# Output products in token layout, a norm as two numbers a partition, and h updated by fp32 products with a diagonal

## The chip, the cores and the metric

The kernel runs on one core of one Trainium2 chip. The metric is the device time of one execution in microseconds (us); lower is better. All inputs lie in the chip's memory (HBM) when it starts. The engines that the text speaks of are TensorE (PE; its weight loads are PEld), VectorE (DVE), ScalarE (ACT), GpSimd (POOL) and SyncE (SP, which issues the weight transfers).

## The reference, cut to what matters

Two residual blocks over 256 tokens of width 2048, all in fp32. `h` is the residual stream; every sublayer has the same frame, of which the change touches the norm ahead of it, its last product, and the update of `h`:

```
rms_norm(x, g) = x * rsqrt(mean(x*x, axis=-1) + 1e-6) * g
h = x
# block 1
z = rms_norm(h, g) @ w_in                     # then a recurrent mixer and sparse attention
h = h + rms_norm(concat(rms_norm(y_lru), rms_norm(y_nsa)) @ w_out, g)
h = h + rms_norm(square(relu(rms_norm(h, g) @ mlp_w1)) @ mlp_w2, g)
h = h + sigmoid(h @ ple_gate) * (p @ ple_proj)
# block 2: layer 0 has the mixer "sb_gla", layer 1 the mixer "s5"
for layer in 0, 1:
    y = mixer(rms_norm(h, g0))                # s5 ends in val * sigmoid(gate), (val, gate) = y @ w_glu
    h = h + rms_norm(y, g1)
    gate, up = split(rms_norm(h, g2) @ w_ffn_in)
    h = h + rms_norm((silu(gate) * up) @ w_ffn_out, g3)
```

So there are six updates of the form `h = h + rms_norm(...)` and six norms of `h` ahead of a product.

## The kernel before, in words

**Layout.** Activations lie transposed: a tile of 128 channels (partitions) by 256 tokens, 16 such tiles k = 0..15 for the width 2048. `h` is `[128, 16, 256]`. An operand of a product is split in two fp32r parts, high and low (`split`, L245 and L246, or with a gain L248 and L249), and a product is the sum of high*high, low*high and high*low.

**Products.** `wload` fetches a piece of the weights (512 KB: two k-tiles of 512 columns), ACT rounds it to `wh` (L261), DVE forms the rest `wl` (L262); there are four buffers of each. `group` makes 512 output columns of a product: for each k, weight tiles of 128x128 are the loaded operand, and the activations stream. In the wide form (used where `self.alt` is set) high and low stream together, 512 columns for `wh` and 256 for `wl`, and each output tile takes a PSUM bank of its own; in the narrow form (around the two mixers, and at the end of an output product) three products of 256 columns each. `evac` empties the banks. `outs` runs `group` four times for an output product (2048 columns); in the last call the last 512 columns are cut in two halves (`narrow`). `agroup` with `amode` is an existing third form, used for a few products in the mixers (L751 to L753): there the activations of 128 tokens are the loaded operand and 512 columns of weights stream, so that the output has tokens on its partitions.

**Banks.** PSUM has eight banks of 512 columns: four called `ps`, two `px`, two `pm`. `group` takes four of `ps` and `px` in a rotation of three patterns (`self.gpar`).

**The boundary between two sublayers.** The output product is evacuated in fp32 into `Y`; ACT squares each tile, DVE adds the squares (`stat`), `rnorm` sums them over partitions by fp32 products with a matrix of ones (L442), and makes the reciprocal root on a 128x256 tile with Ln and Exp on ACT and four DVE operations (L447 to L454). Twenty products without use (`fill`, L430) lie behind the L442. Then `upd(k)`: `t = Y[k] * r` (L533, on DVE, every second one on POOL) and `h[k] += t` (L534, DVE). `make_x` hands out `pre(k)`, which calls `upd(k)` and splits h[k] with the gain; the first `group` of the next sublayer calls `pre(k)` for each k, so its products wait for the tiles one after the other. The norm of the new `h` is taken behind this first group: `h_stat` squares on ACT (L381) and adds on POOL (L382), then `rnorm`, and where a number per token on partitions is wanted, `rnorm_tok` (L461, two products of one column). The result scales the evacuated products, since the norm is one factor per token.

**What sets the order.** Each engine runs its instructions in order. The order is set when the kernel is built, by priorities that follow the program; the work of `s5_gen`, which prepares tables for the s5 mixer mostly on POOL, is given a lower priority and lies between other work.

Of the kernel before, what the change touches and what calls it, by code (L numbers as in the profile page):

```python
# [18 lines left out]
P = 128  # L19
T = 256  # L20
# [115 lines left out]
class K:  # L136
# [195 lines left out]
    def outs(self, Xk, ks, W, r0, last, step=None, tags=("ps",) * 4, **kw):  # L332

        for gi in range(4):
            if step:
                step(gi)
            if not (last and gi == 3):
                yield gi * 4, self.group(Xk, ks, lambda k0: self.wload(  # L340
                    [((slice(None),), self.wsrc(W, r0 + k0 - ks[0], gi * 512))]), tag=tags[gi], **kw)
                continue
            for k in (12, 14):
                yield k, self.group(Xk, ks, lambda k0: self.wload(
                    [((slice(None),), self.wsrc(W, r0 + k0 - ks[0], k * P, 4, T))], (P, 4, T)),
                    ntile=2, kc=4, tag=tags[gi], **{**kw, "narrow": True})
# [36 lines left out]

    def stat(self, acc, y, k):

        if k < 12:
            if k == 0:
                acc.append(self.acct())
            self.sq_add(acc[0], y, k == 0)
        else:  # L390
            acc.append(self.l())
            self.last_act = self.nc.scalar.activation(acc[-1], y, AF.Square)
# [63 lines left out]
    def rnorm_tok(self, acc, n):  # L456

        nc = self.nc
        ps = self.ps()
        for c in range(2):  # L460
            nc.tensor.matmul(ps[:, c:c + 1], acc[:, c * P:(c + 1) * P], self.ones[:, 0:1], start=True, stop=True)  # L461
        v = self.s([P, 16], tag="nv")[:, :2]
        nc.vector.tensor_scalar(v, ps[:, 0:2], 1.0 / n, EPS, op0=ALU.mult, op1=ALU.add)
        r = self.rsqrt_small(v, 2)
        rt = self.s([P, 2], tag="rt")
        nc.vector.tensor_copy(rt, r)
        return rt
# [50 lines left out]
    def h_stat(self):  # L518
        acc = self.acct()
        for k in range(NK):  # L520
            self.sq_add(acc, self.h[:, k], k == 0, self.nc.gpsimd)
        return acc

    def post_norm(self, Y, acc, fill=20):

        nc = self.nc
        r = self.rtile("c")
        self.rnorm(acc, D, r, fill)

        def upd(k, engs=None):  # L530
            t = self.e()
            m, a = engs or (nc.gpsimd if k > 1 and k % 2 else nc.vector, nc.vector)
            m.tensor_tensor(t, Y[:, k], r, op=ALU.mult)  # L533
            a.tensor_tensor(self.h[:, k], self.h[:, k], t, op=ALU.add)  # L534

        return upd

    def newY(self):
        return self.xs([P, NK, T], F32)

    def put_ys(self, Y, acc, k0, ys, gain):

        for i, y in enumerate(ys):
            self.stat(acc, y, k0 + i)
        for i, y in enumerate(ys):
            self.nc.scalar.activation(Y[:, k0 + i], y, AF.Copy, scale=self.vec(gain[0], gain[1] + k0 + i))
# [90 lines left out]
    def block1_in(self):  # L637
# [10 lines left out]
        for gi in range(2):  # L648
            ps = self.group(Xk, ks, std(C_U + gi * 512), pre=pre)
            if pre:  # L650
                pre = None
                acc = self.h_stat()
                self.rnorm(acc, D, rb)
                rt = self.rnorm_tok(acc, D)
# [261 lines left out]
    def nsa_gen(self, q, ksw, vv, kcmp, VB, gt, wk):  # L916
# [141 lines left out]
        self.r_nsa = self.rtile("c")  # L1058
        self.rnorm(acc, 1024, self.r_nsa)
# [6 lines left out]
    def block1(self):  # L1066
# [10 lines left out]
        for k, ps in self.outs(lambda k: XL[:, k], list(range(8)), W, 0, False):  # L1077
            for j, p in enumerate(ps):
                self.evac(p, out=Y[:, k + j])
        acc = []  # L1080
        for k, ps in self.outs(lambda k: self.XN[:, k - 8], list(range(8, 16)), W, 8, True, tags=("ps", "ps", "px", "ps"),
                               pre=self.mix_until(self.made)):
            self.mix_end()
            ys = [self.evac(p, mul=self.r_nsa) for p in ps]
            for j, y in enumerate(ys):
                (nc.gpsimd if k < 12 else nc.vector).tensor_tensor(y, y, Y[:, k + j], op=ALU.add)
            self.put_ys(Y, acc, k, ys, ("mix_post", 0))
# [4 lines left out]
        self.upd = self.post_norm(Y, acc)  # L1092
# [4 lines left out]
    def mlp(self):  # L1097
# [3 lines left out]
        rb = self.rtile("a")  # L1101
        r2 = self.rtile("b")
        W1, W2 = I["mlp_w1"], I["mlp_w2"]
        Y = self.newY()
        accy = []
        ks = list(range(16))
        for ch in range(4):
            H = self.newX()
            self.bg_drain = ch == 3
            for gi in range(4):  # L1110
# [5 lines left out]
                if pre:  # L1116
                    pre = None
                    self.dump("h1", self.h)
                    self.rnorm(self.h_stat(), D, rb)
                    V.tensor_tensor(r2, rb, rb, op=ALU.mult)  # L1120
# [14 lines left out]
            for k, ps in self.outs(lambda k: self.xk(H, k), ks, W2, ch * 16, ch == 3, step):  # L1135
                if ch < 3:
                    for j, p in enumerate(ps):
                        self.evac(p, out=Y[:, k + j], add=Y[:, k + j] if ch else None)
                else:
                    ys = [self.evac(p, add=Y[:, k + j], mul=r2) for j, p in enumerate(ps)]  # L1140
                    self.put_ys(Y, accy, k, ys, ("mlp_post", 0))
        self.ple_proj(0, behind)
        self.upd = self.post_norm(Y, accy, 0)
        self.ple_proj(1)

# [35 lines left out]
    def finish(self):  # L1181
        nc = self.nc
        ov = self.out.rearrange("(k p) t -> p k t", p=P)
        for k in range(NK):
            self.upd(k, ((nc.vector, nc.gpsimd)[k % 3 == 2],) * 2)
# [4 lines left out]
    def mixer0(self):  # L1190
# [12 lines left out]
        for dst, c0, mul in ((gk, 3584, rb), (gq, 3072, r8)):  # L1203
            ps = self.group(Xk, ks, std(c0), pre=pre)
            if pre:
                pre = None
                hd = self.save_h()
                acc = self.h_stat()
# [816 lines left out]
```

## Time and profile before

| | |
|---|---|
| median of 3 runs | 3584.61 us (3579.72 to 3590.34) |
| the profiled execution: time | 3582.63 us |
| its span | 3580.8 us |
| its mean granted clock of TensorE | 0.986 |
| PE busy | 3460.7 us, 97% of the span, 22198 instructions |
| DVE, ACT, POOL busy | 2332.0, 1831.7, 1030.5 us |
| chain that ended last | PE 87%, DVE 6%, ACT 2% |

Read it so: PE is busy nearly all the time, and most of the chain that sets the end is PE's own stream of L304 products. The idle time that PE has lies in a few places, and its boundaries are among them.

### The profile page before, as it was taken

How to read it: one execution, taken by the hardware profiler on the slowest of the kernel's cores; microseconds unless marked ns; L12 is line 12 of the kernel's file. 1: busy time of each engine (PE TensorE's matmuls, PEld its weight loads, DVE VectorE, ACT ScalarE, POOL GpSimd, SP SyncE). 2: the span in 40 equal slices, each digit the busy share in tenths (PEclk: the TensorE clock that was granted, in tenths of full speed). 3: DMA queues.
4: the chain of work that ended last, by engine and by line, in shares of the span. 5: the costliest groups of instructions: out<-in, count | busy, mean ns of one | idle time of the engine just before them, and what ended most of it. 6: DMA issues, size and time to landing. Idle time of an engine off the chain costs nothing.

```text
span 3580.8 us, 59154 instructions
## 1 busy us (share of the span) xinstructions
PE 3460.7 (97%) x22198; PEld 3039.8 (85%) x22198; DVE 2332.0 (65%) x3610; ACT 1831.7 (51%) x2879; POOL 1030.5 (29%) x1510
## 2 busy tenths in 40 slices
PE   9999999999999999999899999999689899999998
PEld 9888888888888898999788888888578888888887
DVE  7686785567656867546766566667755765565557
ACT  5656654644445644346544444445555544444444
POOL 2231242299620113103445565556300200000000
PEclk9999999999999999999999999999899999999999
DMA  8744456667766564566577777778876466666664
GB/s 237 213 121 152 127 176 190 184 216 216 245 206 197 179 195 140 144 196 186 153 217 233 225 238 224 232 223 277 265 223 187 144 190 190 190 189 188 189 189 130
DMA packets 506167, 699.55 MB, mean 195 GB/s; under 512 B 43318, under 2 KB 317143, under 8 KB 505880
## 3 DMA queue, kind: packets, MB, share of 16 engines
q1 hardware_dynamic: 473712, 628.99, 57.2%
q0 software_dynamic: 27456, 63.65, 5.8%
q8 instruction: 174, 2.85, 0.3%
q10 hardware_dynamic: 4712, 3.13, 0.3%
q14 instruction: 113, 0.93, 0.1%
HBM read 654.17 MB, written 37.22 MB: 193 GB/s over the span
## 4 chain that ended last, share of the span: by engine, by line
PE 87%; DVE 6%; ACT 2%; DMA 2%; issue 2%; POOL 2%; SPq 0%; DVEq 0%; ACTq 0%; POOLq 0%
PE ps L304 58%; PE px L304 21%; DVE x L534 1%; DVE wl L262 1%; PE ps L751 1%; PE ps L752 1%; PE ps L753 1%; PE pm L1734 1%; ACT wh L261 1%; DVE e L533 1%; DVE x L249 1%; DMA m<-in_s5bT_dram 0%; DMA m<-in_wg_dram 0%; PE px L973 0%; PE px L1363 0%
## 5 line engine op out<-in xcount | busy, mean ns | idle before, releaser
L262 DVE TENSOR_TENSOR wl<-wr,wh 128x1024 fp32r<-128x1024 f32 x1126 | 1452.4, 1293 | 1070.1 <-ACT wh L261 1062.8
L304 PE MATMUL ps<-x,wh 128*128 128x512 f32 (+1 forms) x8000 | 2080.6, 350 | 33.0 <-DVE x L249 14.1
L261 ACT ACTIVATE wh<-wr 128x1024 fp32r<-128x1024 f32 x1126 | 1188.5, 1058 | 1291.8 <-PE ps L304 775.5
L304 PE MATMUL ps<-x,wl 128*128 128x256 f32 x6272 | 1390.2, 281 | 0.8 <-DVE wl L262 0.7
L304 PEld LDWEIGHTS ps<-x,wl 128*128 128x128 f32 x6272 | 1187.3, 190 | 205.0 <-issue 3.4
L304 PEld LDWEIGHTS ps<-x,wh 128*128 128x128 f32 x8000 | 1241.5, 191 | 52.2 <-DVE x L249 15.2
L304 PE MATMUL px<-x,wh 128*128 128x512 f32 (+1 forms) x2336 | 733.3, 395 | 16.2 <-DVE x L249 14.3
L304 PEld LDWEIGHTS px<-x,wl 128*128 128x128 f32 x2304 | 433.6, 188 | 102.6 <-issue 2.4
L304 PE MATMUL px<-x,wl 128*128 128x256 f32 x2304 | 459.1, 279 | 0.0
L304 PEld LDWEIGHTS px<-x,wh 128*128 128x128 f32 x2336 | 358.6, 189 | 28.0 <-DVE x L249 17.0
L533 POOL TENSOR_TENSOR e<-x,r_c 128x256 f32<-128x256 f32 x40 | 39.7, 997 | 1052.9 <-DVE r_c L454 1044.9
L382 POOL TENSOR_TENSOR acc<-acc,sq 128x256 f32<-128x256 f32 x89 | 78.0, 877 | 246.8 <-ACT sq L381 244.1
L1776 POOL TENSOR_TENSOR m<-m,m 128x128 f32<-128x128 f32 x128 | 69.6, 567 | 242.0 <-PE pm L1734 242.0
L365 ACT ACTIVATE e<-ps 128x256 f32<-128x256 f32 x288 | 106.1, 371 | 51.1 <-PE ps L304 47.9
L245 ACT ACTIVATE x<-e 128x256 fp32r<-128x256 f32 x168 | 67.8, 410 | 78.9 <-DVE e L1513 42.1
L367 DVE TENSOR_TENSOR e<-ps,e 128x256 f32<-128x256 f32 x256 | 105.0, 415 | 4.3 <-ACT e L365 4.3
L1793 POOL TENSOR_TENSOR m<-m,m 128x256 f32<-128x256 f32 x64 | 65.9, 1029 | 73.2 <-DMA m<-in_s5bT_dram 73.1
L246 DVE TENSOR_TENSOR x<-e,x 128x256 fp32r<-128x256 f32 x168 | 78.5, 476 | 12.5 <-ACT x L245 8.8
L1775 POOL TENSOR_TENSOR m<-m,m 128x128 f32<-128x128 f32 x128 | 76.1, 619 | 0.7
L1795 POOL TENSOR_TENSOR m<-m,m 128x256 f32<-128x256 f32 x64 | 72.6, 1134 | 0.7
L365 ACT ACTIVATE e<-px 128x256 f32<-128x256 f32 x144 | 53.4, 370 | 24.5 <-PE px L304 23.0
L751 PE MATMUL ps<-wh,x 128*128 128x512 f32 x160 | 64.4, 403 | 0.3 <-ACT wh L261 0.3
(486 smaller groups left out, 2870.0 us busy)
## 6 DMA issues: line engine op xcount, KB each, us to landing
wr<-in_w_ffn_in_dram SPq DMA_DIRECT2D x704, 256.0 KB, 3.2
wr<-in_mlp_w_dram SPq DMA_DIRECT2D x256, 512.0 KB, 4.2
wr<-in_w_ffn_out_dram SPq DMA_DIRECT2D x176, 512.0 KB, 4.5
wr<-in_w_in_dram SPq DMA_DIRECT2D x152, 512.0 KB, 3.8
wr<-in_w_out_dram SPq DMA_DIRECT2D x64, 512.0 KB, 3.8
wr<-in_w_glu_dram SPq DMA_DIRECT2D x128, 256.0 KB, 3.1
wr<-in_ple_gate_dram SPq DMA_DIRECT2D x32, 512.0 KB, 4.1
wr<-in_w_in_dram SPq DMA_DIRECT2D x32, 256.0 KB, 5.1
```

The source lines that it names most:

```text
L246: b = (eng or nc.vector).tensor_tensor(dst[:, 1], src, dst[:, 0].bitcast(F32), op=ALU.subtract)
L261: nc.scalar.activation(wh, wr, AF.Copy)
L262: nc.vector.tensor_tensor(wl, wr, wh.bitcast(F32), op=ALU.subtract)
L304: mm = lambda o, w, x, a, z: nc.tensor.matmul(o, w, x, start=a, stop=z, skip_group_check=True)
L365: a = S.activation(t, ps[:, T:2 * T], AF.Copy)
L367: self.hold = a, V.tensor_tensor(z, ps[:, 0:T], t, op=ALU.add)
L382: (eng or nc.vector).tensor_tensor(acc, acc, q, op=ALU.add)
L533: m.tensor_tensor(t, Y[:, k], r, op=ALU.mult)
L751: nc.tensor.matmul(ps, xh, wh, start=first, stop=False, skip_group_check=True)
L1775: G_.tensor_tensor(cx[:, q], u_(0), l_(0), op=ALU.mult)
L1776: G_.tensor_tensor(t1[:, q], u_(1), l_(1), op=ALU.mult)
L1795: G_.tensor_tensor(ob[:, :, ri], ob[:, :, ri], t1, op=(ALU.subtract, ALU.add)[ri])
```

## The change

`outs` no longer calls `group`, but a new function `atok`: activations of 128 tokens loaded, weights streaming, as `agroup` does (which now calls it). `Y` becomes `[128 tokens, 2 halves, 2048 channels]`. Two `ps` banks hold a group's output, emptied by one operation each (`add_up`). The squares of a token then lie along a row, and ACT's Square sums them itself (`accum_out`, `sq_sum`): the norm is two numbers on each partition. `rsqrt_tok` makes the reciprocal root on a 128x2 tile (13 DVE operations of two elements; 15 where the factor `by` comes in). `post_norm` writes it on the diagonal of two 128x128 matrices `dg`, and `upd(k)` is two fp32 products, Y's 128x128 block (loaded) with `dg` (streaming), which transpose and scale in one, into a `px` bank, and one DVE operation `h[k] += gain * pt`. The fills are gone, and POOL has no part in an update.

The norm of the new `h` (`h_norm`, at five places: both mixers' entries with `rb` and `rt`, the mlp, and both ffn) is changed too: ACT squares h[k], and two fp32 products of one column sum each square over partitions, 32 products in all. `bcast` spreads the result along a row where it is wanted (`rb`).

The diff, cut to its core:

```diff
+    def atok(self, Xk, ks, load, w, kc=2, pre=None, tag="ps"):
+        pv = [self.ps(tag)[:, 0:w] for _ in range(2)]
+        n = len(ks)
+        for a in range(0, n, kc):
...
+            wh, wl = load(ks[a])
+            for kk in range(kc):
+                for c in range(2):
+                    self.amode(pv[c], Xk(ks[a + kk]), c, wh[:, kk], wl[:, kk], a + kk == 0, a + kk == n - 1)
+            self.mix_step()
+        return pv
...
-                yield gi * 4, self.group(Xk, ks, lambda k0: self.wload(
+                yield slice(gi * 512, gi * 512 + 512), self.atok(Xk, ks, lambda k0: self.wload(
...
+    def rsqrt_tok(self, ss, n, tag="rt", by=None):
+        V = self.nc.vector
         v = self.s([P, 16], tag="nv")[:, :2]
+        if by is not None:
+            V.tensor_tensor(v, ss, by, op=ALU.mult)
+            V.tensor_tensor(v, v, by, op=ALU.mult)
+            ss = v
+        V.tensor_scalar(v, ss, 1.0 / n, EPS, op0=ALU.mult, op1=ALU.add)
         r = self.rsqrt_small(v, 2)
...
-    def h_stat(self):
-        acc = self.acct()
+    def h_norm(self, dst=None, tag="rt"):
+        nc = self.nc
+        ps = self.ps()
         for k in range(NK):
-            self.sq_add(acc, self.h[:, k], k == 0, self.nc.gpsimd)
-        return acc
+            q = self.e("sq", bufs=2)
+            self.last_act = nc.scalar.activation(q, self.h[:, k], AF.Square)
+            for c in range(2):
+                nc.tensor.matmul(ps[:, c:c + 1], q[:, c * P:(c + 1) * P], self.ones[:, 0:1], start=(k == 0 and c == 0),
+                                 stop=(k == NK - 1), skip_group_check=True)
+        rt = self.rsqrt_tok(ps[:, 0:2], D, tag)
+        if dst is not None:
+            self.bcast(rt, dst)
+        return rt
...
-    def post_norm(self, Y, acc, fill=20):
+    def post_norm(self, Y, ss, gain, by=None):
...
-        r = self.rtile("c")
-        self.rnorm(acc, D, r, fill)
-
-        def upd(k, engs=None):
-            t = self.e()
-            m, a = engs or (nc.gpsimd if k > 1 and k % 2 else nc.vector, nc.vector)
-            m.tensor_tensor(t, Y[:, k], r, op=ALU.mult)
-            a.tensor_tensor(self.h[:, k], self.h[:, k], t, op=ALU.add)
+        V.tensor_reduce(s2, ss[:, :, 0:self.ssn], axis=AX.X, op=ALU.add)
+        r = self.rsqrt_tok(s2, D, "rp", by)
+        dg = [self.s([P, P], tag="dg", bufs=2) for _ in range(2)]
+        for c in range(2):
+            V.tensor_scalar(dg[c], self.ident, r[:, c:c + 1], None, op0=ALU.mult)
+        banks = {}
+        self.gpar = 2
+
+        def upd(k, eng=None):
+            if k % 2 == 0:
+                banks[0] = self.ps("px")
+            pt = banks[0][:, (k % 2) * T:(k % 2 + 1) * T]
+            for c in range(2):
+                nc.tensor.matmul(pt[:, c * P:(c + 1) * P], Y[:, c, k * P:(k + 1) * P], dg[c], start=True, stop=True)
+            V.scalar_tensor_tensor(self.h[:, k], pt, self.vec(gain[0], gain[1] + k), self.h[:, k], op0=ALU.mult, op1=ALU.add)
...
-                    self.rnorm(self.h_stat(), D, rb)
+                    rt = self.h_norm(rb, "rf")
...
-            with self.low(-self.bg_low):
+            with self.low(-3 * self.bg_low):
```

The order of PE's instructions moves at two places. The first is the boundary from the s5 mixer's last product to the ffn of layer 1. Before (`pm` sums, `l` squares, `cst` the ones, `px` and `ps` the ffn's output, `x` the activations):

```order
L442 MATMUL pm_29733<-l_29596,cst 128x256
L442 MATMUL pm_29733<-l_29729,cst 128x256
L430 MATMUL pm_29739<-cst 128x128 x20
L304 MATMUL px_29776<-x_29770,wh_29793 128x512
L304 MATMUL px_29777<-x_29770,wh_29793 128x512
L304 MATMUL px_29776<-x_29770,wl_29794 128x256
```

Now (L788 is the third product of `amode`, L577 the update's products, whose loaded operand `x_25870` is Y):

```order
L787 MATMUL ps_27189<-wl_27287,x_25869 128x256
L788 MATMUL ps_27189<-wh_27286,x_25869 128x256
L577 MATMUL px_27363<-dg_27348,x_25870 128x128
L577 MATMUL px_27363<-dg_27349,x_25870 128x128
L577 MATMUL px_27397<-dg_27348,x_25870 128x128
L577 MATMUL px_27397<-dg_27349,x_25870 128x128
L577 MATMUL px_27363<-dg_27348,x_25870 128x128
L577 MATMUL px_27363<-dg_27349,x_25870 128x128
L577 MATMUL px_27397<-dg_27348,x_25870 128x128
L304 MATMUL ps_27359<-x_27352,wh_27377 128x512
```

The sums by ones and the fills are gone; three and a half pairs of update products stand ahead of the ffn's first product, the other twelve and a half stand among its first group.

The second place is behind this first group, where the norm of the new `h` is taken. Before, one L442 stands there, and the second group follows without a break:

```order
L304 MATMUL ps_29779<-x_29771,wl_30025 128x256 x2
L442 MATMUL pm_30091<-acc_30044,cst 128x256
L304 MATMUL ps_30131<-x_29770,wh_30138 128x512 x2
L304 MATMUL ps_30131<-x_29770,wl_30139 128x256 x2
L304 MATMUL ps_30132<-x_29770,wh_30138 128x512 x2
```

Now PE has the one-column products L542 of 15 squares there, one pair at a time between products of the second group (whose banks are `px_27758`, `px_27759`, `ps_27760` and `ps_27761`); the last four pairs:

```order
L542 MATMUL pm_27635<-cst,sq_27684 128x1 x2
L304 MATMUL ps_27760<-x_27352,wl_27789 128x256
L542 MATMUL pm_27635<-cst,sq_27688 128x1 x2
L304 MATMUL ps_27760<-x_27352,wl_27789 128x256
L304 MATMUL px_27758<-x_27352,wh_27811 128x512 x2
L542 MATMUL pm_27635<-cst,sq_27692 128x1 x2
L304 MATMUL px_27758<-x_27352,wl_27812 128x256
L542 MATMUL pm_27635<-cst,sq_27696 128x1 x2
```

and eight rows later the products that spread the norm along a row (L421), and the first product into the last of the second group's banks:

```order
L304 MATMUL px_27759<-x_27352,wh_27834 128x512 x2
L421 MATMUL pm_27722<-dg_27723,cst 128x128
L421 MATMUL pm_27722<-dg_27726,cst 128x128
L304 MATMUL px_27759<-x_27352,wl_27835 128x256 x2
L304 MATMUL ps_27760<-x_27352,wh_27834 128x512 x2
L304 MATMUL ps_27760<-x_27352,wl_27835 128x256 x2
L304 MATMUL ps_27761<-x_27352,wh_27765 128x512 x2
```

On ACT the same place now reads so (`sq` squares of h, L1537 Silu of a gate that the norm has scaled, L261 the rounding of weights, L245 the split of silu(gate)*up, L379 the emptying of a bank; `ps_27360` is the bank that `ps_27761` takes over):

```order
L540 ACTIVATE sq_27696<-x_17191 128x256
L379 ACTIVATE e_27737<-ps_27361 128x256
L1537 ACT_TABLE_LOAD
L1537 ACTIVATE e_27730<-e_27730 128x256
L261 ACTIVATE wh_27857<-wr_27854 128x1024
L245 ACTIVATE x_27357<-e_27740 128x256
L379 ACTIVATE e_27745<-ps_27360 128x256
```

The emptying of `ps_27360` now stands behind a Silu and a split that need the norm. The ffn of layer 0 has the same order at both places.

## Rows read from the trace of the kernel before

**Rows 1.** The page, part 1: busy us of each engine.

```profile
PE 3460.7 (97%) x22198; PEld 3039.8 (85%) x22198; DVE 2332.0 (65%) x3610; ACT 1831.7 (51%) x2879; POOL 1030.5 (29%) x1510
```

**Rows 2.** The chain that ended last: start us, us, what.

```profile
493.38 22.29 PE ps L304 x128
...
1287.57 23.03 PE ps L304 x192
```

**Rows 3.** Busy time in a stretch of agroup's products alone: PE, its clock, DMA.

```profile
1524.73:1551.25 26.52, 26.52 (x118) 1.00 0.75 219
```

**Rows 4.** Timeline of PE: start us, us, what. Short fp32 products among fp32r ones.

```profile
1310.87 0.50 PE L461 MATMUL pm<-cst,acc 128*128 128x1 f32 x4
1311.23 0.48 PE L304 MATMUL ps<-x,wh 128*128 128x256 f32 x2
...
1496.51 0.60 PE L417 MATMUL px<-dg,cst 128*128 128x128 f32 x4
1496.87 0.48 PE L304 MATMUL ps<-x,wh 128*128 128x256 f32 x2
1497.19 0.28 PE L304 MATMUL ps<-x,wl 128*128 128x256 f32 x1
```

**Rows 5.** The same, one-column products whose squares come from ACT just then.

```profile
1457.44 0.40 PE L304 MATMUL ps<-x,wh 128*128 128x256 f32 x2
1457.84 0.61 PE L1402 MATMUL ps<-cst,sq 128*128 128x1 f32 x4
1458.31 0.36 PE L304 MATMUL ps<-x,wl 128*128 128x256 f32 x1
```

**Rows 6.** Timeline of PE, boundary from block 1's mixer to the mlp.

```profile
427.77 0.59 PE L442 MATMUL pm<-acc,cst 128*128 128x256 f32 x2
...
470.30 0.38 PE L442 MATMUL pm<-acc,cst 128*128 128x256 f32 x1
```

**Rows 7.** Timeline of PE and DVE, boundary from the sb_gla mixer to ffn 0.

```profile
1712.27 0.59 PE L442 MATMUL pm<-acc,cst 128*128 128x256 f32 x2
...
1729.79 1.60 DVE L534 TENSOR_TENSOR x<-x,e 128x256 f32<-128x256 f32 x1 [8.39 <-POOL e L533]
...
1763.47 0.70 PE L304 MATMUL ps<-x,wh 128*128 128x512 f32 x2
```

**Rows 8.** Timeline of PE, boundary from the s5 mixer to ffn 1.

```profile
2802.23 0.59 PE L442 MATMUL pm<-l,cst 128*128 128x256 f32 x2
...
2843.29 0.60 PE L442 MATMUL pm<-acc,cst 128*128 128x256 f32 x2
```

**Rows 9.** Timeline of PE, first product of ple.

```profile
1196.74 0.50 PE L304 MATMUL ps<-x,wh 128*128 128x512 f32 x1 [1.08 <-DVE x L246]
```

**Rows 10.** Chain of the boundary from ffn 0 to s5: start us, us, what.

```profile
2524.62 0.67 DVE x L534 x2
...
2539.58 0.71 PE pm L1839 x2
```

**Rows 11.** Timeline at the end of the program: PE's last sums, DVE's last update.

```profile
3558.34 0.59 PE L442 MATMUL pm<-acc,cst 128*128 128x256 f32 x2
...
3577.22 0.42 DVE L534 TENSOR_TENSOR x<-x,e 128x256 f32<-128x256 f32 x1
```

**Rows 12.** Stretches: PE, PEld, DVE, ACT, POOL busy, PE's granted clock, DMA.

```profile
1736.00:1738.00 2.00, 2.00 (x12) 1.78 (x12) 2.00 (x6) 0.73 (x3) 0.81 (x1) 0.93 0.00 0
3568.00:3570.00 2.00, 0.00 (x0) 0.00 (x0) 2.00 (x3) 0.00 (x0) 1.84 (x3) 0.81 0.39 131
```

**Rows 13.** Small operations on DVE (timeline), and groups by line on ACT.

```profile
1317.53 0.16 DVE L406 SCALAR_TENSOR_TENSOR ny<-nt,ny 128x2 f32<-128x2 f32 x1
1317.72 0.17 DVE L466 COPY rt<-ny 128x2 f32<-128x2 f32 x1
...
L248 ACT ACTIVATE x<-x,vec 128x256 fp32r<-128x256 f32 x83 | 40.1, 503 | 46.5 <-DVE x L534 43.5 <-DVE x L1179 2.7
```

**Rows 14.** Groups by line and form on PE: count, busy us, mean ns, idle before and releasers.

```profile
L304 PE MATMUL ps<-x,wh 128*128 128x512 f32 x4544 | 1439.0, 398 | 24.6 <-DVE x L249 14.1 <-DVE e L367 4.7 <-ACT wh L261 2.4
```

More of the change, by code (lines that the diff above doesn't have):

```diff
@@ L536, in post_norm @@
         return upd
     def newY(self):
[L539 to L546, printed above, removed]
+        return self.xs([P, 2, D], F32)
     def softplus_neg_small(self, x, n):
@@ L1076, in block1 @@
             self.put_xn(t, y)
[L1077 to L1082, printed above, removed]
+        for cols, pv in self.outs(lambda k: XL[:, k], list(range(8)), W, 0, False):
+            for c in range(2):
+                nc.scalar.activation(Y[:, c, cols], pv[c], AF.Copy)
+        ss = self.sums()
+        for cols, pv in self.outs(lambda k: self.XN[:, k - 8], list(range(8, 16)), W, 8, True, pre=self.mix_until(self.made)):
             self.mix_end()
[L1084 to L1087, printed above, removed]
+            for c in range(2):
+                y = Y[:, c, cols]
+                nc.vector.scalar_tensor_tensor(y, pv[c], self.r_nsa[:, c:c + 1], y, op0=ALU.mult, op1=ALU.add)
+                self.sq_sum(ss, y, c)
         self.alt = True
@@ L1133, in step, with add_up @@
                     self.bg_clean()
[L1135 to L1141, printed above, removed]
+            for cols, pv in self.outs(lambda k: self.xk(H, k), ks, W2, ch * 16, ch == 3, step):
+                self.add_up(Y, cols, pv, ch, ss if ch == 3 else None)
         self.ple_proj(0, behind)
-        self.upd = self.post_norm(Y, accy, 0)
+        self.upd = self.post_norm(Y, ss, ("mlp_post", 0), r2)
         self.ple_proj(1)
+    def add_up(self, Y, cols, pv, add, ss):
+        for c in range(2):
+            y = Y[:, c, cols]
+            if add:
+                self.nc.vector.tensor_tensor(y, pv[c], y, op=ALU.add)
+            else:
+                self.nc.scalar.activation(y, pv[c], AF.Copy)
+            if ss is not None:
+                self.sq_sum(ss, y, c)
     def ple_proj(self, half, behind=None):
@@ L1257, in mixer0 @@
         Y = self.newY()
-        for k, ps in self.outs(lambda k: XG[:, k - 8], list(range(8, 16)), W, 8, False):
-            for j, p in enumerate(ps):
-                self.evac(p, out=Y[:, k + j])
-        acc = []
-        for k, ps in self.outs(lambda k: XS[:, k], list(range(8)), W, 0, True, pre=self.mix_until(self.made)):
+        for cols, pv in self.outs(lambda k: XG[:, k - 8], list(range(8, 16)), W, 8, False):
+            self.add_up(Y, cols, pv, False, None)
+        ss = self.sums()
+        for cols, pv in self.outs(lambda k: XS[:, k], list(range(8)), W, 0, True, pre=self.mix_until(self.made)):
             self.mix_end()
-            ys = [self.evac(p, add=Y[:, k + j]) for j, p in enumerate(ps)]
-            self.put_ys(Y, acc, k, ys, ("ng2", 16))
+            self.add_up(Y, cols, pv, True, ss)
         self.alt = True
@@ L1515, in ffn @@
             last = k_lo + nk == 44
-            for k, ps in self.outs(lambda k: self.xk(H, k), list(range(nk)), W2, k_lo, last, lambda gi: self.bg_step(2)):
-                if not last:
-                    for j, p in enumerate(ps):
-                        self.evac(p, out=Y[:, k + j], add=Y[:, k + j] if k_lo else None)
-                else:
-                    ys = [self.evac(p, add=Y[:, k + j], mul=rb) for j, p in enumerate(ps)]
-                    self.put_ys(Y, accy, k, ys, ("ng2", layer * 64 + 48))
+            for cols, pv in self.outs(lambda k: self.xk(H, k), list(range(nk)), W2, k_lo, last, lambda gi: self.bg_step(2)):
+                self.add_up(Y, cols, pv, k_lo, ss if last else None)
             k_lo += nk
         self.bg_end()
-        self.upd = self.post_norm(Y, accy)
+        self.upd = self.post_norm(Y, ss, ("ng2", layer * 64 + 48), rt)
     def s5_gen(self):
```

105 lines of the change are left out of this document (49 added, 56 removed).

## The prediction

> **What bounds the kernel now.** I read the page first: PE is busy 97% of the span [rows 1], so a change counts where it shortens PE's stream or the stretches in which PE stands. Next the chain that ended last: it is made of long runs of L304. A wide group is 128 products in 22.29 us, 1.393 us for each k; a narrow one 192 products in 23.03 us, 1.439 us for each k [rows 2]. Then the stretch in which agroup runs alone, which is the form that all output products get: 117 steps from the first to the last product start in 26.52 us, 0.2267 us each at the full clock [rows 3]; six of them make a k, 1.360 us. Last the boundaries, where PE waits for the chain norm, update of h, split. From the previous product's end to the end of the first group (the 128th product) they take 42.5 us into the mlp [rows 6], 51.3 into ffn 0 [rows 7] and 41.1 into ffn 1 [rows 8], against 22.3 for the group alone. Into ffn 0 DVE once waits 8.39 us for POOL, which has other work queued ahead of its part of the update [rows 7].
>
> **The change part by part: what the token layout gives.** The number of columns that stream is the same; the gain is only the difference in pace. Wide k's that change form: mlp 15 groups of 16 (240), each ffn 164 (four groups of 16 k, four of 16, three of 12), the s5 mixer's last product 112: 680 in all, times 1.393 - 1.360 = 0.033 us, 22.4 us. Narrow k's around the mixers: 7 half groups of 8 k at two places, 112 times 0.079, 8.8 us. The last 512 columns of each product stream 256 at a time before and after and give nothing. Together **-31.2 us**. It is paid fully, since PE is the bound there; the emptying of banks gets lighter on DVE and ACT, which hides behind PE either way.
>
> **What the short fp32 products cost.** Two fp32 products of 128 columns (four records) hold PE from 1496.51 to 1496.87, and the two products behind them start the next 0.32 apart where 0.24 (two of 23.03/192 = 0.12) is usual: 0.36 + 0.08 = 0.44 us a pair [rows 2, 4]. Two of one column: 1310.87 to 1311.23, again 0.36, and the same 0.08 [rows 4]. So a pair costs 0.44 with 128 columns or with one. The 16 pairs of an update, and the 16 of a norm, are 7.0 us of PE each. The lower bound for the one-column pair is the 0.08, if its loads hide; the upper 0.55, the 0.47 of a pair whose squares come just then with the 0.08 [rows 5]. I take 0.44, since the order sets the pairs singly among fp32r products, as in rows 4.
>
> *Entries of the two mixers* (norm only). PE is the bound, the 16 pairs add 7.0; gone are one L442 and one L461 pair (0.43 + 0.44), new is the spreading pair (0.44): +6.6 at the second. At the first three pairs stand where PE still waits for the first weights: +5.3.
>
> *mlp to ple.* The products of ple_proj cover the chain, and PE waits 1.08 us for its first tile [rows 9], 1.4 in all with a later 0.3. The update's pairs add 7.0 to a PE that is the bound: +5.6.
>
> *Into mlp, ffn 0, ffn 1.* Chain now, from the last product: one 128x256 DVE operation of 0.42 [rows 11], Square with its sum 0.6, the reduce 0.2, 13 small DVE operations at 0.19 to 0.2 from start to start [rows 13] 2.6, two diagonals 0.6, a pair 0.5, update 0.45, split on ACT 0.5 [rows 13] and on DVE 0.45, latencies 0.4: 6.7. Then the group, 22.3; the twelve and a half pairs that the order puts among it, 5.5; for the clock 1.8 (with the fills gone PE stands some 5 us; after the wait into ffn 0 it ran at half clock from its restart at 1732 until the slice 1736 to 1738, whose mean is 0.93, four us at half [rows 12]); 1.0 for waits between tiles, now that POOL has no part and DVE needs about 1.5 us a tile (update 0.45, split 0.43, half a weight load 0.65) against PE's 1.83. The norm's pairs behind it 7.0. Sum 44.3. Before, 42.5 and one L442 of 0.43, so into the mlp: +1.4.
>
> In both ffn's there is more: the spreading pair 0.44, and a new wait. The order puts the emptying of `ps_27360` on ACT behind a Silu that needs the new norm; before PE may start on `ps_27761` (the same bank) these must pass behind the last one-column pair: 13 small operations 2.6 and diagonals 0.6, the spreading pair 0.5, copy 0.45, scaling 0.43, Silu 0.4, ACT's weight rounding 1.06, split 0.4, copy out of the bank 0.4, DVE's half 0.5 with what DVE has queued, about 8.5 in all, under which PE has eight rows and three more, about 4 us of products. I take 4.4 of standing. What is queued behind it is PE's whole stream. Sum 49.1: against 41.1 + 0.43 +7.6 into ffn 1, against 51.3 (its L442 lies inside) -2.2 into ffn 0, where POOL's 8.39 us is what is won.
>
> *ffn 0 to s5.* ACT bounds the 16 tiles, from the first new h at 2525.3 to PE's last sum at 2539.6 [rows 10]. The first h now comes 5.7 us behind the last product, 3.9 earlier than before (it came 9.6 behind). What follows waits partly for transfers of tables; between 0 and -3.9 I take -2.
>
> *End of the program.* From PE's first sum to DVE's last update 19.3 us, then 3.2 of output to the span's end [rows 11]. Now 5.0 of chain, updates of 0.45 on DVE, and the first of them at half clock (the slice 3568 to 3570 shows 0.81 as PE stands [rows 12]): 4 us for the first four and a half updates, 5.2 for the rest, 0.5 to end, 3.2: 17.9 (18.4 with some waiting) against 22.5. **-4**.
>
> *Banks.* An output group needs two `ps` banks; where the group ahead holds four (six places) PE may wait for DVE. Before, all waits of this kind were 4.7 us [rows 14]. Bounds 0 and 6; I take +2. The move of s5_gen's products and of table loads on ACT is costed at nothing: PE does the same products, and ACT has slack; uncovered it is one table load, about a us.
>
> **Sum.** -31.2 + 5.3 + 6.6 + 5.6 + 1.4 - 2.2 + 7.6 - 2 - 4 + 2 = -10.9. The profiled execution took 3582.63, so 3571.7, **3572 us**; that execution is 2 us under the median of the runs. What a measurement can tell from no change is about 0.3%, 10.75 us.
>
> **A rule weighed against the rows.** The one-column pair costs 0.36 + 0.08 here [rows 4], as much as one of 128 columns, so its loads are not hidden. The Trainium skill, TensorE: Matmul & The Clock Gate, section Step-by-step: what each phase is for, says that weight loads are pulled ahead of running products, so that the next tile's load lies under this one's streaming. In rows 4 that does not hold for a pair's four records in a row, but there the neighbours stream 256 columns, and now many stream 512. By rows 4 the sum stays 3572; by the rule it would be the 3543 of the first rival.
>
> **The rivals.** *The loads hide.* If the loads of a one-column pair lie under the 512-column neighbours, it costs only the 0.08: 80 pairs times 0.36 is 28.8 less, 3543 us. For it: an L304 product hides its own load. Against it: rows 4. Chance 0.10.
>
> *The boundaries take all.* PE stands longer in both ffn's (DVE's weight rest of 1.2 us in between, and the clock falls again, 2 us each), and the bank waits reach 6: about 3 + 4 + 4 more, 3582. For it: a wait of 8.39 at such a boundary did drop the clock [rows 7, 12]. Against it: little is queued on DVE at this place in the order. Chance 0.18.
>
> *Each pair waits for its square* (the slower one). Only two buffers hold squares, so a Square on ACT waits for PE's pair two before, and PE's in-order stream waits for the Square. ACT squares in 0.4 but rounds weights in 1.06 between. In rows 5 such a pair had PE wait 0.16 us ahead of it. The change is worth nothing when a pair costs 0.44 + 10.9/80 = 0.58, and is slower by 0.3% from 0.71; at 0.75 it is 3597. Against it: the order leaves 0.35 us or more of other products between two pairs. Chance 0.17.
>
> **How the numbers follow.** The forecast has 0.55, and its own range is 3562 to 3582; its part below 3573.9 (10.75 under the median) is 0.33, the rest 0.22 is no change. The hidden loads add 0.10 to faster; the second rival 0.02 faster, 0.15 same, 0.01 slower; the third 0.03 same and 0.14 slower. Faster 0.45, same 0.40, slower 0.15. The range 3552 to 3592 leaves out most of the first rival and over half of the third.
>
> **What would show each step.** L786 to L788 start 0.227 us apart in all output products; L542 pairs lengthen PE's stream by 0.44 each (0.08 or 0.7 by the rivals); the first group into the mlp ends about 37 us behind the last product; in both ffn's PE stands about 4 us behind L421, waiting for DVE's emptying; nothing on POOL in an update. Wrong would be the prediction if output products ran at another pace than agroup's, or if ACT's order of squares and weight rounding left PE without weights.

## The result, and the profile after

The changed kernel takes **3618.43 us** (median of 4 runs, 3615.51 to 3620.52) against 3583.97 for the kernel before (4 runs beside it). The ratio is 1.0094, 95% interval 1.0077 to 1.0112: slower by 34 us. The prediction said 3572, with 3592 as the upper end. The profiled execution took 3617.48, its span is 3615.7 and its mean granted clock 0.983 (before: 0.986).

From the page of the changed kernel, the busy times that answer to [rows 1], and the chain that ended last:

```profile
PE 3485.3 (96%) x20610; PEld 2998.3 (83%) x20610; DVE 2152.0 (60%) x3323; ACT 1737.1 (48%) x2621; POOL 904.5 (25%) x1378
...
PE 85%; POOL 5%; DVE 4%; DMA 3%; ACT 2%; issue 1%; SPq 0%; ACTq 0%; DVEq 0%; POOLq 0%
PE ps L304 34%; PE px L304 11%; PE ps L786 11%; PE ps L788 11%; PE ps L787 11%; POOL m L1737 1%; POOL m L1738 1%; POOL m L1739 1%; PE px L577 1%; PE pm L1756 1%; DMA TBd<-m 1%; DVE wl L262 1%; ACT wh L261 1%; PE pm L542 0%; DMA m<-in_wg_dram 0%
```

The chain before, by engine:

```profile
PE 87%; DVE 6%; ACT 2%; DMA 2%; issue 2%; POOL 2%; SPq 0%; DVEq 0%; ACTq 0%; POOLq 0%
```

DVE, ACT and POOL have less to do than before, yet POOL's share of the chain went from 2% to 5%. Its lines there, L1737 to L1739, are those of s5_gen, which the change was not about.

To see where the time came from, the execution is cut at the same eight places in both traces: the ends of the last output products, the first product of ple_proj, the thin product of mixer 0, the first product of the s5 mixer's last stage (glu). The change that the prediction had for each piece is the sum of its own terms (mlp: +1.4 and 240 k at 0.033; ffn 0 with s5: -2.2, -2 and 164 k; ffn 1: +7.6 and 164 k; glu: 112 k; the +2 for banks has no place):

| stretch | before, us | after, us | change | predicted |
|---|---|---|---|---|
| start to w_out's end | 427.9 | 431.7 | +3.8 | +0.9 |
| mlp, to ple_proj | 753.9 | 773.7 | +19.8 | -6.5 |
| ple, and mixer 0's entry | 152.5 | 172.0 | +19.5 | +12.2 |
| mixer 0 | 378.1 | 374.4 | -3.7 | -4.4 |
| ffn 0 and s5, to glu | 907.8 | 909.8 | +2.0 | -9.6 |
| glu | 182.2 | 177.8 | -4.4 | -3.7 |
| ffn 1 | 756.1 | 756.0 | -0.1 | +2.2 |
| end | 22.3 | 20.2 | -2.1 | -4.0 |

The last three pieces and mixer 0 came as forecast within 2.3 us. The mlp is 26 off, ffn 0 with s5 12, ple 7, the start 3.

**The mlp.** The timeline of PE and POOL in the changed kernel (start us, us, what, and in brackets the idle time ahead and who ended it):

```profile
880.27 0.39 PE L304 MATMUL px<-x,wl 128*128 128x256 f32 x2
...
890.08 1.25 POOL L1799 TENSOR_TENSOR m<-m,m 128x512 f32<-128x512 f32 x1
...
891.39 0.63 PE L1756 MATMUL pm<-m,m 128*32 128x128 f32 x2 [10.72 <-POOL m L1799]
...
895.57 1.26 POOL L1799 TENSOR_TENSOR m<-m,m 128x512 f32<-128x512 f32 x1
...
896.89 0.42 PE L1756 MATMUL pm<-m,m 128*32 128x128 f32 x1 [2.85 <-POOL m L1799]
```

PE comes to s5_gen's first short products at 880.66, and POOL ends the two sums that they need at 891.33 and 896.83. PE's stream is in order, so all its products stand behind. Where PE restarts, the granted clock is 0.50 and a short pair takes 0.56 us instead of 0.33; the stream is back at 903.48, 22.8 us after it stopped, for a step that takes 4 elsewhere (979.7 to 983.8). That is 18.8 us lost, and the clock stays at 0.50 until 908.4, which costs some 2 more. Before, the same step stood one group of products later, where POOL had long been done:

```profile
879.57 1.28 POOL L1777 TENSOR_TENSOR m<-m,m 128x512 f32<-128x512 f32 x1
...
887.46 1.30 POOL L1777 TENSOR_TENSOR m<-m,m 128x512 f32<-128x512 f32 x1
...
903.66 0.42 PE L1734 MATMUL pm<-m,m 128*32 128x128 f32 x6
```

**The entry of ple.** The timeline of SP, ACT and PE in the changed kernel:

```profile
1200.67 0.37 SPq L1188 DMA_DIRECT2D m<-in_pT_dram x1
...
1201.84 0.40 ACT L556 ACTIVATE m<-x 128x256 f32<-128x256 f32 x1
...
1204.90 0.42 ACT L245 ACTIVATE m<-m 128x256 fp32r<-128x256 f32 x1 [2.57 <-DMA m<-in_pT_dram]
...
1205.37 1.14 PE L304 MATMUL ps<-m,wh 128*128 128x256 f32 x3 [4.93 <-ACT m L245]
```

PE has done its last output product at 1200.44. What ple_proj multiplies (pT) is only fetched at 1200.67, into one of nine rotating buffers `m`; the squares that `sq_sum` throws away (L556) go to the same nine. Before, ple_proj's products followed the last output product without a gap, at 1181.84.

### The profile page after: what moved, and what is told of

Read it like the earlier page. It is cut to its first block, busy times and chain, and to the rows that moved or that the text cites. A ratio compares the mean times of both kernels' runs of the same rounds, so it can differ in the third digit from the quotient of the medians.

```text
span 3615.7 us, 55161 instructions
## 1 busy us (share of the span) xinstructions
PE 3485.3 (96%) x20610; PEld 2998.3 (83%) x20610; DVE 2152.0 (60%) x3323; ACT 1737.1 (48%) x2621; POOL 904.5 (25%) x1378
## 4 chain that ended last, share of the span: by engine, by line
PE 85%; POOL 5%; DVE 4%; DMA 3%; ACT 2%; issue 1%; SPq 0%; ACTq 0%; DVEq 0%; POOLq 0%
PE ps L304 34%; PE px L304 11%; PE ps L786 11%; PE ps L788 11%; PE ps L787 11%; POOL m L1737 1%; POOL m L1738 1%; POOL m L1739 1%; PE px L577 1%; PE pm L1756 1%; DMA TBd<-m 1%; DVE wl L262 1%; ACT wh L261 1%; PE pm L542 0%; DMA m<-in_wg_dram 0%
## 5 line engine op out<-in xcount | busy, mean ns | idle before, releaser
L261 ACT ACTIVATE wh<-wr 128x1024 fp32r<-128x1024 f32 x1126 | 1190.4, 1058 | 1441.0 <-PE ps L788 538.4
L304 PE MATMUL ps<-x,wh 128*128 128x512 f32 (+1 forms) x4864 | 1285.9, 353 | 12.8 <-DVE e L381 4.6
L304 PE MATMUL ps<-x,wl 128*128 128x256 f32 x3840 | 856.5, 283 | 1.5 <-DVE wl L262 1.5
L304 PEld LDWEIGHTS ps<-x,wl 128*128 128x128 f32 x3840 | 729.5, 191 | 130.3 <-issue 5.5
L304 PEld LDWEIGHTS ps<-x,wh 128*128 128x128 f32 x4864 | 760.8, 192 | 29.0 <-issue 10.8
L786 PE MATMUL ps<-wh,x 128*128 128x512 f32 (+1 forms) x2032 | 768.4, 378 | 5.6 <-ACT wh L261 3.6
L787 PE MATMUL ps<-wl,x 128*128 128x512 f32 (+1 forms) x2032 | 762.7, 375 | 0.8 <-DVE wl L262 0.8
L788 PE MATMUL ps<-wh,x 128*128 128x512 f32 (+1 forms) x2032 | 762.3, 375 | 0.0
L786 PEld LDWEIGHTS ps<-wh,x 128*128 128x128 f32 x2032 | 383.1, 189 | 79.5 <-ACT wh L261 4.1
L788 PEld LDWEIGHTS ps<-wh,x 128*128 128x128 f32 x2032 | 383.1, 189 | 70.3 <-issue 2.0
L787 PEld LDWEIGHTS ps<-wl,x 128*128 128x128 f32 x2032 | 383.5, 189 | 69.0 <-issue 1.8
L304 PE MATMUL px<-x,wh 128*128 128x512 f32 x1280 | 404.9, 397 | 1.8 <-DVE e L381 1.8
L304 PE MATMUL px<-x,wl 128*128 128x256 f32 x1280 | 256.0, 280 | 0.3 <-DVE wl L262 0.3
L245 ACT ACTIVATE x<-e 128x256 fp32r<-128x256 f32 x168 | 68.3, 411 | 87.9 <-DVE e L1540 48.7
L577 PE MATMUL px<-dg,x 128*128 128x128 f32 x384 | 62.8, 309 | 29.7 <-DVE dg L568 28.7
L577 PEld LDWEIGHTS px<-dg,x 128*128 128x128 f32 x384 | 56.6, 216 | 33.7 <-DVE dg L568 21.0
```

Of the source, the lines that this page charges most:

```text
L245: a = nc.scalar.activation(dst[:, 0], src, AF.Copy)
L261: nc.scalar.activation(wh, wr, AF.Copy)
L304: mm = lambda o, w, x, a, z: nc.tensor.matmul(o, w, x, start=a, stop=z, skip_group_check=True)
L577: nc.tensor.matmul(pt[:, c * P:(c + 1) * P], Y[:, c, k * P:(k + 1) * P], dg[c], start=True, stop=True)
L786: nc.tensor.matmul(ps, xh, wh, start=first, stop=False, skip_group_check=True)
L787: nc.tensor.matmul(ps, xh, wl, start=False, stop=False, skip_group_check=True)
```

## The experiments

Each was run beside the kernel before on the same chip, and ratios are to that kernel. A difference between two ratios is given in us of 3584.

**1. s5_gen's products back at their place (e1_late_products).**

```diff
-            with self.low(-3 * self.bg_low):
+            with self.low(-self.bg_low):
```

> The changed kernel with one edit undone: the eight short products of each step of s5_gen get back the place in PE's stream that they have in the kernel before (an offset of -100 instead of -300). Theory: in the changed kernel they stand one group earlier, before GpSimd has what they multiply; PE then stands 10.72 and 2.85 us for it in the mlp at 880 to 897 and restarts at the lower clock, 18.8 us in all against the 4 us that six such steps take elsewhere. With the edit undone that stretch shrinks: no PE wait of over 3 us for L1799 in the mlp, and the time falls from 3618 by 15 to 20, to 3598 to 3603. Rival: GpSimd itself is some 10 us later than before (its first L1799 ends at 891.3 instead of 880.9), so PE meets the wait at the later place as well and gains less than 5: 3613 to 3618. Second rival: later products hold up the tables behind them, and the s5 mixer loses what the mlp wins: 3615 to 3622.

Measured: 3593.39, ratio 1.0033 (1.0022 to 1.0045). Against 1.0094 that is 0.61%, 22 us less. The timeline of POOL and PE there:

```profile
896.42 1.28 POOL L1799 TENSOR_TENSOR m<-m,m 128x512 f32<-128x512 f32 x1
...
903.02 2.29 POOL L1799 TENSOR_TENSOR m<-m,m 128x512 f32<-128x512 f32 x1
...
905.36 0.41 PE L1756 MATMUL pm<-m,m 128*32 128x128 f32 x2 [0.20 <-POOL m L1799]
```

POOL is even later here, but PE comes at 904.75 and waits 0.20. The first theory holds; both rivals are out. The mlp with the gap into ple takes 753.4 instead of 773.7.

**2. A scratch of its own for the squares (e2_own_scratch).**

```diff
-        ... activation(self.m([P, 512])[:, 0:y.shape[-1]], y, AF.Square, ...
+        ... activation(self.e("l", (P, 512), mybir.dt.bfloat16, bufs=7)[:, 0:y.shape[-1]], y, AF.Square, ...
```

> The changed kernel with one edit: the squares that sq_sum throws away (only their sum is kept) go to a scratch buffer of the kind l, as bfloat16, instead of to the rotating buffers m, which the transfer of pT also takes its place from. Theory: pT's transfer is now issued only at 1200.67, behind the last Square of the mlp's output, since it has to wait for an m buffer; PE stands 4.93 us for its rounding and restarts at the lower clock (about 1.7 us more). With the edit the transfer is issued many groups earlier, PE starts ple_proj at once behind the last output product, and the norm's chain lies under ple_proj's products: 6 to 9 us less, 3609 to 3612. Rival: the norm's chain (first update at 1218.5) is then what PE waits for, since it no longer lies under the wait: less than 3 us gained, 3615 to 3618.

Measured: 3607.36, ratio 1.0082 (1.0055 to 1.0109), which overlaps the changed kernel's interval: alone it decides nothing. In its trace pT's transfer is issued at 1016.4 instead of 1200.67 and the wait at ple's entry is gone, but the one for POOL in the mlp is longer (12.82 and 2.87 us instead of 10.72 and 2.85), and the mlp stretch is 775.9.

**3. Both (e3_both).**

> Both edits together (the products of s5_gen at their place before, and a scratch of its own for the squares). If the two waits are separate, the gains add: 21 to 29 us less than 3618, 3589 to 3597, so that the kernel is within about 0.3% of the one before. If GpSimd is late for a reason that both share (the m buffers that its tiles and the squares take turns in), the sum is less than the parts by 5 us or more.

Measured: 3581.45, ratio 1.0000 (0.9985 to 1.0016). Against experiment 1 this is 0.33%, some 12 us for the scratch (by the two intervals 5 to 19, so the 6 to 9 expected are not excluded): besides the gap at ple's entry (5.34 us in experiment 1, none here) ffn 0 with s5 got shorter, 895.7 instead of 902.6. Together the two edits account for the whole 34 us by which the change was slower. They do not give the 11 us by which it was to be faster.

**4. One-column products doubled (e4_double_columns).** On the changed kernel.

```diff
-            for c in range(2):
-                nc.tensor.matmul(ps[:, c:c + 1], q[:, c * P:(c + 1) * P], ...
+            for c in range(4):
+                a = c % 2 * P
+                nc.tensor.matmul(ps[:, c:c + 1], q[:, a:a + P], ...
```

> The changed kernel with the one-column products of h_norm doubled: each square is multiplied four times instead of twice, the second pair into two columns that nobody reads. 80 pairs more. By the price that the prediction used (0.44 us a pair, 0.36 of it between neighbours) the time rises by 29 to 35, to 3647 to 3653. If loads of a one-column product hide under the 512-column neighbours, it rises by about 6, to 3625. A look at the second mixer: the granted clock was 0.50 at 1356 to 1360 while PE was busy with such products and the narrow products among them; if the one-column products are what lowers it, the stretch at the lower clock grows and the time rises by some us more.

Measured: 3708.79, ratio 1.0362 (1.0337 to 1.0387): 96 us more than the changed kernel, 1.2 for each added pair. In the changed kernel itself a pair costs what the prediction said while the clock is full (timeline of PE: 0.36 from the first of four records to the next product, as in [rows 4]):

```profile
1346.02 0.50 PE L542 MATMUL px<-cst,sq 128*128 128x1 f32 x4
1346.38 0.36 PE L304 MATMUL ps<-x,wl 128*128 128x256 f32 x1
```

What came on top is the clock. Stretches of mixer 0's entry (PE, PEld, DVE, ACT, POOL busy, PE's granted clock, DMA share, GB/s); first the changed kernel:

```profile
1348.00:1352.00 4.00, 4.00 (x37) 4.00 (x37) 1.01 (x1) 2.82 (x6) 0.00 (x0) 1.00 0.32 116
1356.00:1360.00 4.00, 4.00 (x20) 4.00 (x20) 1.53 (x6) 2.32 (x3) 0.00 (x0) 0.50 0.00 0
```

and with the products doubled:

```profile
1388.00:1396.00 8.00, 8.00 (x39) 8.00 (x39) 0.00 (x0) 1.67 (x4) 0.00 (x0) 0.50 0.00 0
1396.00:1404.00 8.00, 8.00 (x39) 8.00 (x39) 1.22 (x1) 2.20 (x4) 0.00 (x0) 0.50 0.18 18
```

PE stands nowhere in these stretches, and the clock is at its lower level, 1.2 GHz (0.50), all the same. With the products doubled it stays there for longer at the entries of the two mixers (27 and 31 us, at 41 to 68 and 1386 to 1416, instead of 3.4 and 6.8), and it falls at those of the mlp (501 to 518), ffn 0 (1860 to 1880) and ffn 1 (2949 to 2980 with a break), where it had held. An estimate from these stretches: some 113 us more at half the pace are 56 lost, and 80 pairs at 0.44 are 35, together 91 of the 96.

**5. The sum on GpSimd (e5_sums_on_gpsimd).** On experiment 3.

```diff
-        ps = self.ps()
+        acc = self.acct()
         for k in range(NK):
-            q = self.e("sq", bufs=2)
-            self.last_act = nc.scalar.activation(q, self.h[:, k], AF.Square)
-            for c in range(2):
-                nc.tensor.matmul(ps[:, c:c + 1], q[:, c * P:(c + 1) * P], self.ones[:, 0:1], ...
...
-        rt = self.rsqrt_tok(ps[:, 0:2], D, tag)
+            self.sq_add(acc, self.h[:, k], k == 0, self.nc.gpsimd)
+        rt = self.rnorm_tok(acc, D, tag)
```

> On top of the version with both edits (products of s5_gen late, a scratch of its own), the norm of h goes back to adding the 16 squares on GpSimd and making two one-column products at the end, in place of 32 one-column products. Theory: 75 pairs fewer at 0.36 to 0.44 us each give 27 to 33 us, and the stretch in the second mixer at half the clock (1329 to 1346 in that version, about 8 us lost) goes too: 35 to 41 less than 3581, 3540 to 3546. Rival: the sum is late again (16 additions at 0.88 us on GpSimd, which also works for s5_gen), the emptying of the banks behind the norm waits, and under 15 us are left: 3566 or more.

Measured: 3555.30, ratio **0.9927** (0.9908 to 0.9947), 26 us less than experiment 3 by the ratios and 35 by the two profiled spans (3586.1 and 3550.7). It is the best version: 0.7% faster than before and 1.7% faster than the changed kernel. The rival is out. The size by the ratios (by the two intervals 17 to 35) lies below the range expected and is about that of the pairs alone; its trace shows the full clock at mixer 0's entry.

**6. The update's products doubled (e6_double_update).** On experiment 3.

```diff
-            for c in range(2):
+            for c in (0, 0, 1, 1):
                 nc.tensor.matmul(pt[:, c * P:(c + 1) * P], Y[:, c, k * P:(k + 1) * P], dg[c], ...
```

> On top of the version with both edits, every product of an update of h with the diagonal is made twice into the same place, 80 pairs of 128 columns more. By the prediction's price of 0.44 us a pair the time rises by 35 us, to 3616. If such products lower the clock as the doubled one-column ones did (96 us for 80 pairs instead of 29 to 35), it rises by 70 to 100. If they hide, by less than 10.

Measured: 3628.02, ratio 1.0129 (1.0109 to 1.0148), 46 us more. There are six updates, so 96 pairs were added, not the 80 of the expectation: 0.48 a pair, close to 0.44, and the clock stays (mean 0.984 against 0.982 in experiment 3).

**7. The kernel before, with the early products alone (e7_before_early_products).** The edit of experiment 1 the other way round, in the old code.

> The kernel before with one edit of the change alone: the short products of s5_gen one group earlier in PE's stream (offset -300). Theory of the early products: PE comes to them at 882 instead of 903.7, GpSimd's two sums end at 880.9 and 888.8, so PE stands some 6 us for the second, once, with perhaps 2 us for the clock: 3587 to 3590 against 3581. Rival: the price of 20 us in the changed kernel belongs to this edit alone whatever the rest: 3598 to 3602. Second rival: in the kernel before the edit costs nothing: 3581.

Measured: 3609.31, ratio 1.0076 (1.0047 to 1.0105): 27 us slower. The interval, 17 to 38 us, leaves out the theory's 6 to 9 and the second rival's 0; the first rival's 17 to 21 lie at its lower end. Two of the four runs took 3599 and 3602, two 3616 and 3618, and the trace is from one of the longer two. Timeline of PE:

```profile
878.34 0.39 PE L304 MATMUL px<-x,wl 128*128 128x256 f32 x2
887.04 0.64 PE L1734 MATMUL pm<-m,m 128*32 128x128 f32 x2 [8.30 <-POOL m L1777]
...
892.55 0.64 PE L1734 MATMUL pm<-m,m 128*32 128x128 f32 x2 [2.86 <-POOL m L1777]
```

PE came 3 us sooner and POOL's first sum 6 later (886.98) than worked out from the kernel before; a wait of 5.26 us for DVE at 1022.5 is new too, and ffn 0 with s5 takes 914.8 instead of 907.8. So this one offset costs 22 of the 34 us that the change lost, and 27 in the old code.

**8. 128 columns of ones instead of one (e8_wide_ones).** On experiment 3.

```diff
-                nc.tensor.matmul(ps[:, c:c + 1], q[:, c * P:(c + 1) * P], self.ones[:, 0:1], ...
+                nc.tensor.matmul(ps[:, c * P:(c + 1) * P], q[:, c * P:(c + 1) * P], self.ones, ...
...
-        rt = self.rsqrt_tok(ps[:, 0:2], D, tag)
+        rt = self.rsqrt_tok(ps[:, 0:T:P], D, tag)
```

> On top of the version with both edits, the norm's products multiply each square by 128 columns of ones instead of one (the sum comes out 128 times, one is read). By the prediction's rows a pair of 128 columns costs the same 0.44 as a pair of one column, so as to the stream nothing changes: 3578 to 3584. If the one column is what lets the clock fall in the second mixer (1329 to 1346 at half), the clock stays at 1.00 there and the time falls by about 8 us, to 3571 to 3576. If the additional columns cost time of their own (127 columns at four records a pair are 0.2 us a pair at the full clock), the time rises by 17, to 3598.

Measured: 3577.57, ratio 0.9986 (0.9976 to 0.9996). The intervals of this and of experiment 3 overlap, so the 5 us between them are not settled by the times. The norm's products in mixer 0's entry, first experiment 3, then this one, then experiment 2, which has one column and the same order as experiment 3:

```profile
1332.00:1336.00 4.00, 4.00 (x21) 4.00 (x21) 0.00 (x0) 0.62 (x2) 0.00 (x0) 0.50 0.35 33
1336.00:1340.00 4.00, 4.00 (x20) 4.00 (x20) 0.00 (x0) 1.25 (x3) 0.00 (x0) 0.50 0.00 0
```

```profile
1316.00:1320.00 4.00, 4.00 (x31) 3.44 (x31) 1.23 (x1) 2.56 (x7) 0.00 (x0) 1.00 0.67 194
1320.00:1324.00 4.00, 4.00 (x32) 3.41 (x30) 0.00 (x0) 2.66 (x7) 0.00 (x0) 1.00 0.17 64
```

```profile
1352.00:1356.00 4.00, 4.00 (x38) 4.00 (x36) 0.20 (x1) 2.09 (x6) 0.00 (x0) 1.00 0.61 183
1356.00:1360.00 4.00, 4.00 (x37) 4.00 (x36) 1.23 (x1) 2.40 (x5) 0.00 (x0) 1.00 0.17 17
```

With 128 columns the clock stays at 2.4 GHz (1.00), and the stretch of ple and mixer 0's entry is 169.8 us instead of 175.1. This alone does not show that the columns did it. In experiment 2 the clock stayed at 1.00 with one column, in the same order of PE (167.7 us); it fell there in the changed kernel and in experiments 1, 3, 4 and 6. And the wide products stand in another order, two pairs at a time. That one-column products lower the clock is shown by experiment 4; when a single set of them does so stays open. The 127 more columns cost little: two pairs in a row hold PE for 0.92 us here (1316.64 to 1317.56) and for 0.81 in experiment 2 (1349.80 to 1350.61).

## Why the prediction was wrong, point by point

**The step that failed** is "The move of s5_gen's products and of table loads on ACT is costed at nothing: PE does the same products". The products are the same, their place is not. The prediction named no work that hides the move, and did not set PE's arrival there (880) against POOL's (880.9 and 888.8 before). Experiments 1 and 7 price it at 22 and 27 us.

**What it left out** is the second buffer. Nothing in the sum asked what `sq_sum`'s scratch takes a turn from: "mlp to ple" assumed that ple_proj covers the chain, which needs pT to be there. Experiment 3 against 1: about 12 us, of which the traces show 5.3 as the wait at ple's entry. With both waits gone, experiment 3 is level with the kernel before and not 11 us faster. A misread row (2.8 in the sum), the low clock at mixer 0's entry (8.5 us) and PE's waits in ple (3.0), all below, are of that size; no run took each of them away alone.

**The pace was right.** In the mlp's second chunk the first of 384 output products starts at 727.96, and the next group behind them at 815.03:

```profile
727.96 0.40 PE L786 MATMUL ps<-wh,x 128*128 128x512 f32 x1
...
815.03 0.62 PE L304 MATMUL ps<-x,wh 128*128 128x512 f32 x2
```

87.07/384 = 0.2267 us, as in [rows 3]. In experiment 8, with neither wait, the mlp takes 747.3, 6.6 less than before, where -6.5 was predicted. That it fits to a tenth is luck: experiment 3, without the two waits too, takes 752.9, 3.8 of the difference in short waits of PE between 708 and 902. Glu's -4.4 stands against -3.7.

**The pairs were right** at the full clock: 0.36 to the next product for one column (experiment 4's rows), as in [rows 4], and 0.48 in all for 128 (experiment 6). The first rival, hidden loads, is out, and so is the rule that was weighed with it: beside 512 columns a pair still holds PE for 0.36 (445.85 to 446.21 at the mlp's entry). The third rival did not come either; no PE wait for a Square is among the changed kernel's gaps over 0.1 us. But the price was taken as independent of what runs around it: in the changed kernel the clock is low from 1355.5 to 1362.3, some 3.4 us lost, in experiment 3 from 1329.4 to 1346.5, some 8.5.

**The boundaries.** One row was misread. Into ffn 0 the kernel before takes 48.1 us, not 51.3. Timeline of PE:

```profile
1760.14 0.40 PE L304 MATMUL ps<-x,wl 128*128 128x256 f32 x2
1760.38 0.60 PE L442 MATMUL pm<-acc,cst 128*128 128x256 f32 x2
1760.62 0.81 PE L304 MATMUL px<-x,wh 128*128 128x512 f32 x2
```

The first group's 128 products all go to `ps`, and the last of them ends at 1760.54, 48.1 behind the last output product (1712.43). The products to `px` behind the L442 are the second group's; the prediction counted them in. With 48.1 its own working gives +0.6 for this boundary in place of -2.2, and -8.1 in place of -10.9 for the whole.

Timeline of PE in the changed kernel, entries of the mlp and of ffn 0:

```profile
437.12 3.45 PE L577 MATMUL px<-dg,x 128*128 128x128 f32 x14 [5.42 <-DVE dg L568]
...
481.11 0.49 PE L304 MATMUL ps<-x,wh 128*128 128x512 f32 x1
...
1760.34 3.42 PE L577 MATMUL px<-dg,x 128*128 128x128 f32 x14 [8.53 <-DVE dg L568]
...
1831.17 0.73 PE L304 MATMUL px<-x,wh 128*128 128x512 f32 x2 [1.28 <-DVE e L381]
```

Into the mlp the last product ended at 431.70. At 481.11, behind the norm's last pair, 29 products of the next group are done too; without them (29 at 0.174) the boundary is 44.4 us, and 44.3 was predicted. That the group alone would end 37 behind the last product was off (471.9, 40.2), since the order mixes the norm's pairs into it. Into ffn 0 the wait for the chain is 8.53 instead of 5: the small DVE operations took longer there (last section). Of "4.4 of standing" behind the spreading pair only 2.1 came in ffn 0 (0.27, 1.28 and 0.55) and 0.5 in ffn 1. The end of the program gained 2.1 instead of 4.

**ple.** Of the +17.3 that experiment 8 still has there, 12.2 were predicted, with no wait of PE left. The update's pairs come in four bursts, and PE stands 0.75 us for DVE's split behind each (3.0 in all, 1.6 before). The other 2 us were not taken apart, nor were the 7 us by which ffn 0 with s5 gained from each edit; experiment 7 shows only that the offset costs the same 7 there in the old code. Why POOL ends its first sum at 880.9, 887.0, 891.3 or 897.7 in four kernels with the same work for it stays open too; the runs show only that the early place is ahead of all four and the late place behind them.

## What to carry to other kernels

A change of an order's offset is a change of its own: for each instruction moved on an in-order engine, set its new arrival against the time at which its operands are ready in the trace, before calling it free. A scratch that nobody reads still takes a turn in its pool, and the next transfer into that pool waits for it. Where many tiny sums are taken on the matrix engine, add on an engine with time to spare first and take one product at the end (26 us here).

## What was not expected of the hardware

**The clock falls while PE is busy.** TensorE was busy 4.00 of 4.00 us and granted 0.50 (rows of experiments 4 and 8), among products of 256 columns and loads for one column. Doubling the one-column products made it fall at three more entries. It does not fall each time: in experiment 2 it was granted 1.00 among the same products. The Trainium skill, TensorE: Matmul & The Clock Gate, section What's actually happening, says that the gate goes by how busy the PE has been recently; in these rows it fell although the profile, which counts a one-column product as a quarter of a microsecond, shows PE busy throughout.

**Small DVE operations beside GpSimd.** DVE's chain into ffn 0 in the changed kernel, with POOL at work until 1758.28, and in experiment 3, where POOL waited for a transfer from 1737.8 to 1741.5:

```profile
1754.77 1.84 DVE L402 TENSOR_SCALAR yi<-nv 128x2 int32<-128x2 int32 x1
1756.64 0.32 DVE L403 TENSOR_SCALAR yi<-yi 128x2 int32<-128x2 int32 x1
...
1757.00 1.28 POOL L1799 TENSOR_TENSOR m<-m,m 128x512 f32<-128x512 f32 x1
...
1757.19 1.11 DVE L408 SCALAR_TENSOR_TENSOR nt<-nt,nv 128x2 f32<-128x2 f32 x1
```

```profile
1738.96 0.17 DVE L402 TENSOR_SCALAR yi<-nv 128x2 int32<-128x2 int32 x1
...
1739.57 0.16 DVE L408 SCALAR_TENSOR_TENSOR nt<-nt,nv 128x2 f32<-128x2 f32 x1
...
1741.49 0.76 POOL L1782 TENSOR_TENSOR m<-m,s5rp 128x128 f32<-128x128 f32 x2 [3.68 <-DMA m<-in_s5cb_dram]
```

An operation on two numbers a partition took 1.84 us instead of 0.17 with POOL at work, and PE's wait was 8.53 instead of 5.5. No run here took POOL's work away at that place alone, but the rest of the trace says the same. Of the 227 operations of this size in the changed kernel eight took over 0.25 us, all eight beside an operation of POOL. One of them, and the operation of POOL that it ends with (386.68 and 386.65):

```profile
385.92 0.73 POOL L396 TENSOR_TENSOR acc<-acc,sq 128x256 f32<-128x256 f32 x1 [15.22 <-ACT sq L395]
...
386.01 0.67 DVE L1020 TENSOR_SCALAR mx<-mx 128x2 f32<-128x2 f32 x1
```

The Trainium skill, GPSIMD Engine Reference, section 1. Specifications, says that GpSimd's interfaces to SBUF are shared with VectorE, with contention for DVE instructions that have two inputs there or run in a two-port mode. The rows agree with that for L408, which reads two tiles; L402 and L1020 read one, and no row shows in which mode they ran.
